# The output projection by seven half-size products, with six of the eight merges added by accumulating DMAs

## The chip, the cores and the metric

The kernel runs on one core of one Trainium2 chip. The metric is the device time of one execution in microseconds. TensorE (PE) multiplies, VectorE (DVE) and ScalarE (ACT) do elementwise work, GpSimd (POOL) does a little of it and issues some DMAs, SyncE (SP) only issues DMAs.

## The reference, cut to what matters

One decoder block on 512 tokens of 1024 channels, in float32. Two attention branches read the same normalised input; each is gated, projected to 1024 channels, scaled by a sigmoid gate, and the two are added. One more projection and the residual end it:

```
merged = (jax.nn.sigmoid(ga + b_gate[layer, 0]) * (y_fox @ w_fox[layer])
          + jax.nn.sigmoid(gb + b_gate[layer, 1]) * (y_moba @ w_moba[layer]))
x = x + merged @ w_out[layer]
```

The change concerns the second addend of `merged`, the sum of both, and the last line: a product of 512 x 1024 by 1024 x 1024.

## The kernel before, in words

**Precision.** Every large product is made of three: each operand is split into a high part (`hi`, rounded to the matmul's type by a copy on ACT) and a low part (`lo`, the difference, on DVE), and hi·hi, hi·lo and lo·hi are accumulated in PSUM. `split` (L131) does this for a weight chunk of 128 x 4 x 256 elements, with ACT at L134 and DVE at L136. Weight chunks come in by SP into four slots (`wr`), their parts live in four slots each (`wh`, `wl`).

**Stages.** After the input projections and the attention (until about 291 us) comes the gates stage. It makes the four blocks GA0, GA1, GB0 and GB1 of the sigmoid gates, each by seven products of half the size instead of eight (`group`, L703; the matmuls at L747 to L750 have 256 columns). The sums and differences of activations that this form needs were made earlier; those of weights are DVE subtractions at L711. Between these blocks the MoBA branch is projected: `unit_m` (L807), for i = 0 to 3 (weights wm0 to wm3) and c = 0 and 1, makes one tile j = 2i + c of 128 channels by 512 tokens with `br_mm` (L676 to L678, 12 matmuls of 512 columns). DVE multiplies it by its gate (L813), adds the other branch's gated tile `FS` (L814), ACT makes the high part (L819), DVE the low part (L820). These eight pairs `MG[j]` are the left operand of the output product.

**The output product.** `first_o` (L824) and `unit_o` (L838) multiply the merged tiles by w_out, in four groups of 256 columns (wo0 to wo3) and four tiles of 128 tokens, over 8 tiles of k, three matmuls each of 256 columns: L832 to L834 for the first group, L847 to L849 for the others. `out_o` (L853) loads the piece of x by SP, adds it on DVE (L857) and stores 128 x 256 elements by ACT's queue (L858). PSUM banks have names: `pj` (2), `tp` (3), `lg` (2), `pv` (1).

**The order.** The code is written in the order of the lists at its end (`order`, `seq`, `filler`); `pump` (L179) issues loads when a slot is free and splits weights three units ahead. The framework then orders each engine's instructions by that order and by a planner's costs: an instruction whose operands are not ready in its plan lets a later one of the same engine go first. So matmuls of the first output group stand between branch products in the trace. Each engine then works through its queue strictly in that order and waits where an operand is late. `tc.issue_after` puts instructions behind a given one of their engine. Tiles of a stage's pool lie where those of the stage before lay, and wait for the last user of these bytes.

Of the kernel before, what the change touches and what calls it, by code (L numbers as in the profile page):

```python
# [19 lines left out]
CW = 256  # L20
# [3 lines left out]
WR = 4  # L24
# [5 lines left out]
def fox_moba_kernel(ctx: ExitStack, tc, xT, x, w_in, w_fl, w_fox, w_moba, w_out, cst, rope, out):  # L30


    nc = tc.nc
    V, A, G, T = nc.vector, nc.scalar, nc.gpsimd, nc.tensor

    con = ctx.enter_context(tc.tile_pool(name="con", bufs=1))
    sb = ctx.enter_context(tc.tile_pool(name="sb", bufs=1))
# [3 lines left out]
    stage = {}  # L41
# [46 lines left out]
    cs = con.tile([P, C_END], F32, name="cs")  # L88
# [17 lines left out]
    for i in range(WARM):  # L106
# [10 lines left out]
    Gh = con.tile([P, KT, S], F32R, name="Gh")  # L117
    Gl = con.tile([P, KT, S], F32R, name="Gl")
# [10 lines left out]
    chunks = {}  # L129

    def split(src, n, name, half=False):  # L131
        hi = sb.tile([P, 4, 264], F32R, name=f"wh_{name}", tag="wh", bufs=4)
        lo = sb.tile([P, 4, 264], F32R, name=f"wl_{name}", tag="wl", bufs=4)
        A.activation(hi[:, :, 0:n], src, AF.Copy)  # L134
        for eng, q in ((V, slice(0, 2)), (G, slice(2, 4))) if half else ((V, slice(0, 4)),):
            eng.tensor_tensor(out=lo[:, q, 0:n], in0=src[:, q], in1=hi[:, q, 0:n].bitcast(F32), op=OP.subtract)  # L136
        return hi, lo
# [24 lines left out]
    COLS = {}  # L162
# [13 lines left out]
    loads, preps, first_prep = [], [], {}  # L176
    done = {"loads": 0, "preps": 0}

    def pump(i):  # L179

        while True:
            j = done["loads"]
            if j < len(loads) and (j < WR or loads[j - WR][1] < done["preps"]):
                loads[j][0]()
                done["loads"] += 1
            elif done["preps"] < len(preps) and done["preps"] <= i + 3:
                preps[done["preps"]]()
                done["preps"] += 1
            else:
                return  # L190

    def stream(name):
        first_prep[name] = len(preps)
        if name[0] == "G":
            group(name)
            return
        w, n, cnt = ((w_fox, int(name[2]), 1) if name[:2] == "wf" else (w_moba, int(name[2]), 1) if name[:2] == "wm"
                     else (w_out, int(name[2]), 2) if name[:2] == "wo" else (w_in, COLS[name] // CW, 2))
# [15 lines left out]
    r = con.tile([P, NT], F32, name="r")  # L214
# [33 lines left out]
    HT = S // 2  # L248
# [420 lines left out]
    FS, MG = {}, {}  # L669

    def br_mm(p, name, br, c):
        hi, lo = chunks[name][0]
        cc = slice(c * P, (c + 1) * P)
        for k in range(4):
            yh, yl = Y[br, k]
            T.matmul(p, hi[:, k, cc], yh, start=(k == 0), stop=False)  # L676
            T.matmul(p, hi[:, k, cc], yl, start=False, stop=False)  # L677
            T.matmul(p, lo[:, k, cc], yh, start=False, stop=(k == 3))  # L678
# [14 lines left out]
    SG = {}  # L693
# [7 lines left out]
    groups = {}  # L701
# [104 lines left out]

    def unit_m(i, c):  # L807
        def go():
            j = 2 * i + c
            p = pj(f"pm{j}")  # L810
            br_mm(p, f"wm{i}", "m", c)
            u = SG[i][:, c, :]
            V.tensor_tensor(out=u, in0=p, in1=u, op=OP.mult)  # L813
            V.tensor_tensor(out=u, in0=u, in1=FS[i][:, c, :], op=OP.add)  # L814
# [4 lines left out]
            A.activation(mh_, u, AF.Copy)  # L819
            V.tensor_tensor(out=ml_, in0=u, in1=mh_.bitcast(F32), op=OP.subtract)  # L820
            MG[j] = (mh_, ml_)
        return go

    def first_o():  # L824
        banks = [pst(tg, 2, f"po0_{i}") for i, tg in enumerate(("pj", "pj", "lg", "lg"))]
        for kk in range(KT):
            hi, lo = chunks["wo0"][kk // 4]
            gh, gl = MG[kk]
            k = kk % 4
            for t in range(NT):  # L830
                st = slice(t * P, (t + 1) * P)
                T.matmul(banks[t][:, :CW], gh[:, st], hi[:, k, :CW], start=(kk == 0), stop=False)  # L832
                T.matmul(banks[t][:, :CW], gh[:, st], lo[:, k, :CW], start=False, stop=False)
                T.matmul(banks[t][:, :CW], gl[:, st], hi[:, k, :CW], start=False, stop=(kk == KT - 1))  # L834
        for t in range(NT):
            out_o(banks[t], 0, t)

    def unit_o(n, t):  # L838
        def go():
            p = pj(f"po{n}{t}")  # L840
            st = slice(t * P, (t + 1) * P)
            for hf in range(2):
                hi, lo = chunks[f"wo{n}"][hf]
                for k in range(4):
                    kk = 4 * hf + k
                    gh, gl = MG[kk]
                    T.matmul(p[:, :CW], gh[:, st], hi[:, k, :CW], start=(kk == 0), stop=False)  # L847
                    T.matmul(p[:, :CW], gh[:, st], lo[:, k, :CW], start=False, stop=False)  # L848
                    T.matmul(p[:, :CW], gl[:, st], hi[:, k, :CW], start=False, stop=(kk == KT - 1))  # L849
            out_o(p, n, t)  # L850
        return go

    def out_o(p, n, t):  # L853
        xr = t2("pt", 4, "xr")[:, :CW]
        nc.sync.dma_start(out=xr, in_=x[t * P:(t + 1) * P, n * CW:(n + 1) * CW])
        o = t2("u", 4, "ot")
        V.tensor_tensor(out=o[:, :CW], in0=p[:, :CW], in1=xr, op=OP.add)  # L857
        nc.scalar.dma_start(out=out[t * P:(t + 1) * P, n * CW:(n + 1) * CW], in_=o[:, :CW])  # L858


    order = ["fqa", "fka", "fza", "fzb", "fva", "fqb", "fkb", "fvb", "mqa", "mka", "mva", "mza", "mqb", "mkb", "mvb", "mzb", "wf0", "wf1", "wf2", "wf3",
             "GA0", "GA1", "GB0", "wm0", "wm2",
             "GB1", "wm1", "wm3", "wo0", "wo1", "wo2", "wo3"]
    for nm in order[2:]:
        stream(nm)

    def units(name):
        k = name[:2]
        if k[0] == "G":
            return groups[name]  # L870
        if k == "wf":
            return [unit_f(int(name[2]), c) for c in range(2)]
        if k == "wm":
            return [unit_m(int(name[2]), c) for c in range(2)]
        if k == "wo":
            return [unit_o(int(name[2]), t) for t in range(4)]
# [28 lines left out]
    def seq(names):  # L905
        for u in filler(names):
            u()
# [32 lines left out]
    for n in range(4):  # L940
# [9 lines left out]
        if n == 0:  # L950
            for k in range(4):
                store = []

                at = 3 * k + 5
# [89 lines left out]
```

## Time and profile before

| | us |
|---|---|
| median of 3 runs | 432.96 (432.49 to 433.72) |
| the profiled execution, own time | 432.8 |
| its span, first to last instruction | 431.1 |
| busy in the span: PE, DVE, ACT, POOL | 424.4, 308.5, 253.9, 87.8 |
| last matmul issued | 427.3 |
| last branch matmul (wm3) issued | 383.7 |

The span leaves out what lies before the first and behind the last instruction, so it is 1.7 us shorter than the execution's own time. A matmul's duration in a row is that of one matmul through a pipeline and includes its drain; what matters is the distance between the starts of two in a row. In a row of a stage the granted clock of TensorE is given with 1.00 as full speed. A row of DMA issues ends with the size of one and the median time from issue to landing.

### The profile page before, as it was taken

What the parts mean: (1) busy time and instruction counts of PE and PEld (TensorE: products, weight loads), DVE (VectorE), ACT (ScalarE), POOL (GpSimd) and SP (SyncE); (2) the same over time, 40 slices, a digit from 0 to 9 for tenths busy, and PEclk for the clock granted to TensorE, in tenths of its full rate; (3) what the DMA queues carried; (4) which work ended last, traced back from release to release, by engine and by line L of the source; (5) the groups of instructions that cost most, each with busy time, mean ns of one, the idle gap of its engine ahead of it and who ended that gap; (6) DMA issues with size and microseconds to landing.
All of it is one profiled execution on the core that took longest, in us unless ns stands there. A gap on an engine that the chain in (4) does not pass through costs nothing.

```text
span 431.1 us, 8090 instructions
## 1 busy us (share of the span) xinstructions
PE 424.4 (98%) x3103; PEld 400.7 (93%) x3103; DVE 308.5 (72%) x551; ACT 253.9 (59%) x488; POOL 87.8 (20%) x108
## 2 busy tenths in 40 slices
PE   8999999999999999999999999999999999999996
PEld 6998899999999998999998888899999989999996
DVE  5669976869979867767856896859897796673311
ACT  4986336876867867667765876647645545531100
POOL 1049200227044650045630103020000000000000
PEclk9999999999999999999999999999999999999999
DMA  7981235236565414304304305271415206525231
GB/s 239 398 296 57 80 116 152 74 103 205 166 209 185 130 45 123 122 3 126 117 15 136 109 13 200 99 263 51 141 55 196 98 2 210 189 95 166 85 94 45
DMA packets 25670, 56.13 MB, mean 130 GB/s; under 512 B 3240, under 2 KB 11872, under 8 KB 25632
## 3 DMA queue, kind: packets, MB, share of 16 engines
q1 hardware_dynamic: 14528, 40.08, 27.8%
q10 hardware_dynamic: 9952, 11.34, 8.8%
q0 software_dynamic: 1152, 4.19, 2.7%
q8 instruction: 24, 0.39, 0.4%
q14 instruction: 14, 0.11, 0.1%
HBM read 46.01 MB, written 6.32 MB: 121 GB/s over the span
## 4 chain that ended last, share of the span: by engine, by line
PE 84%; DVE 7%; DMA 5%; ACT 2%; issue 1%; SPq 1%; DVEq 0%; ACTq 0%
PE pb_GB L750 3%; PE pb_GA L750 3%; PE pb_GA L747 3%; PE pb_GB L749 3%; PE pb_GB L747 3%; PE pb_GA L749 3%; PE po L847 3%; PE po L849 3%; PE po L848 3%; PE pv L608 2%; PE pv L607 2%; PE lg L553 2%; PE lg L552 2%; PE pm L676 2%; PE pm L677 2%; PE pm L678 2%
## 5 line engine op out<-in xcount | busy, mean ns | idle before, releaser
L331 POOL TENSOR_TENSOR ff<-ss,mh 128x8 f32<-128x8 f32 x16 | 28.6, 1793 | 65.6 <-DVE ss L329 65.1
L557 ACT ACTIVATE p<-p,negm 128x128 f32<-128x128 f32 (+1 forms) x64 | 35.7, 559 | 9.7 <-DVE negm L555 8.2
L555 DVE CUSTOM_DVE_ANT_0 p<-lg,mask 128x128 f32<-128x128 f32 (+1 forms) x64 | 30.9, 485 | 14.4 <-PE lg L553 13.7
L847 PE MATMUL po<-wh_wo,mgh 128*128 128x256 f32 x96 | 27.1, 282 | 0.0
L849 PE MATMUL po<-wh_wo,mgl 128*128 128x256 f32 x96 | 27.0, 282 | 0.0
L848 PE MATMUL po<-wl_wo,mgh 128*128 128x256 f32 x96 | 27.0, 281 | 0.0
L857 DVE TENSOR_TENSOR ot<-po,xr 128x256 f32<-128x256 f32 x16 | 6.6, 424 | 24.7 <-PE po L849 23.5
L136 DVE TENSOR_TENSOR wl_GA<-wr_ga,wh_GA 128x1024 fp32r<-128x1024 f32 x14 | 17.9, 1294 | 5.7 <-ACT wh_GA L134 3.6
L134 ACT ACTIVATE wh_wo<-wr_wo 128x1024 fp32r<-128x1024 f32 x8 | 8.5, 1061 | 21.6 <-PE po L849 8.0
L552 PE MATMUL lg<-KH,QS 128*128 128x128 f32 (+1 forms) x64 | 20.5, 329 | 0.0
L134 ACT ACTIVATE wh_GA<-wr_ga 128x1024 fp32r<-128x1024 f32 x14 | 14.6, 1059 | 9.2 <-PE pb_GA L749 4.6
L136 DVE TENSOR_TENSOR wl_GB<-wr_gb,wh_GB 128x1024 fp32r<-128x1024 f32 x14 | 16.8, 1222 | 4.2 <-ACT wh_GB L134 3.3
L134 ACT ACTIVATE wh_GB<-wr_gb 128x1024 fp32r<-128x1024 f32 x14 | 14.6, 1060 | 8.6 <-PE pm L677 2.5
L633 DVE TENSOR_TENSOR ypair<-pv,ysh 64x512 f32<-64x512 f32 x16 | 11.0, 688 | 11.2 <-ACT ysh L632 11.0
L847 PEld LDWEIGHTS po<-wh_wo,mgh 128*128 128x128 f32 x96 | 18.1, 189 | 0.0
L848 PEld LDWEIGHTS po<-wl_wo,mgh 128*128 128x128 f32 x96 | 18.1, 189 | 0.0
L849 PEld LDWEIGHTS po<-wh_wo,mgl 128*128 128x128 f32 x96 | 18.1, 188 | 0.0
L136 DVE TENSOR_TENSOR wl_wo<-wr_wo,wh_wo 128x1024 fp32r<-128x1024 f32 x8 | 9.8, 1222 | 7.4 <-ACT wh_wo L134 7.4
L604 DVE TENSOR_TENSOR ptl<-p_a,pth 128x512 fp32r<-128x512 f32 x16 | 11.0, 686 | 4.7 <-ACT pth L603 4.7
L526 DVE SCALAR_TENSOR_TENSOR QS<-p_qT,cs,QS 64x512 fp32r<-64x512 f32 x16 | 12.0, 750 | 2.5 <-ACT QS L525 2.1
L750 PE MATMUL pb_GA<-Gh,wl_GA 128*128 128x256 f32 x48 | 13.6, 283 | 0.0
L749 PE MATMUL pb_GA<-Gl,wh_GA 128*128 128x256 f32 x48 | 13.5, 281 | 0.0
(447 smaller groups left out, 1764.5 us busy)
## 6 DMA issues: line engine op xcount, KB each, us to landing
wr_ga<-in_w_in_dram SPq DMA_DIRECT2D x8, 512.0 KB, 3.5
wr_gb<-in_w_in_dram SPq DMA_DIRECT2D x8, 512.0 KB, 4.1
wr_wo<-in_w_out_dram SPq DMA_DIRECT2D x8, 512.0 KB, 3.8
xt<-in_xT_dram SPq DMA_DIRECT2D x8, 256.0 KB
x<-in_x_dram SPq DMA_DIRECT2D x8, 256.0 KB, 7.5
KH<-KH ACTq DMA_DIRECT2D x16, 128.0 KB, 2.4
s_dramh<-sum_sh ACTq DMA_DIRECT2D x8, 256.0 KB
s_draml<-sum_sl ACTq DMA_DIRECT2D x8, 256.0 KB, 3.5
```

The costliest lines, as they stand in the source:

```text
L134: A.activation(hi[:, :, 0:n], src, AF.Copy)
L136: eng.tensor_tensor(out=lo[:, q, 0:n], in0=src[:, q], in1=hi[:, q, 0:n].bitcast(F32), op=OP.subtract)
L331: G.tensor_tensor(out=f2, in0=ss.rearrange("p t h -> p (t h)"), in1=mh, op=OP.pow)
L552: T.matmul(lg[:, :n], qs[:, qt], kh[:, :n], start=True, stop=False)
L555: V.tensor_tensor_reduce(pt, lg[:, :n], mask[:, 512 - n:512], -0.125, 3.0e38, op0=OP.add, op1=OP.min, accum_out=mkn[:, hh, i:i + 1])
L557: A.activation(pt, pt, AF.Exp, bias=mkn[:, hh, i:i + 1], scale=-1.0, accum_out=rs[:, hh, i:i + 1])
L747: T.matmul(o, hi[:, k, cc], lh, start=(n < 3 and c == 0 and k == 0), stop=False, skip_group_check=True)
L749: T.matmul(o, hi[:, k, cc], ll, start=False, stop=False, skip_group_check=True)
L750: T.matmul(o, lo[:, k, cc], lh, start=False, stop=(k == 3), skip_group_check=True)
L847: T.matmul(p[:, :CW], gh[:, st], hi[:, k, :CW], start=(kk == 0), stop=False)
L848: T.matmul(p[:, :CW], gh[:, st], lo[:, k, :CW], start=False, stop=False)
L849: T.matmul(p[:, :CW], gl[:, st], hi[:, k, :CW], start=False, stop=(kk == KT - 1))
```

## The change

The output product is made in blocks. The merged tiles, as a matrix of tokens by channels, fall into four blocks A11 to A22 (256 tokens by 512 channels), w_out into B11 to B22 (512 by 512). Seven block products replace eight, with sums of left blocks S1 = A21 + A22, S2 = S1 - A11, S4 = A12 - S2, S3 = A11 - A21 and, of weights, T1 = B12 - B11, T3 = B22 - B12, T2 = B22 - T1 and T4 = B21 - T2. Each product is two tiles of 128 tokens, four of k, three matmuls of 512 columns.

- **Merges.** For wm0, wm1 and wm2 the other branch's tile is added by a DMA from GpSimd's queue that accumulates onto the tile in SBUF; for wm3 DVE adds as before. For j < 4 only the first 256 tokens are split into hi and lo (`merge_b`), for j > 3 all 512.
- **Left sums.** `sum_o` makes each sum on DVE for two tiles at once (512 elements), m = 0 from wm0 and wm2, m = 1 from wm1 and wm3; `parts_o` splits it on ACT and DVE into the space of `Gh` and `Gl`, the normalised input's parts, which the gates stage read last.
- **Weights.** Each block is two chunks of 128 x 1024. B11 and B21 come through the `wr` slots, B22 and B12 into the last stage's pool. T1 and T3 are made by a negation on ACT and an accumulating DMA from DRAM; T2 and T4 by DVE subtractions. `prep(n)` splits the weights of product n.
- **Results.** `keep` copies a partial result from PSUM by ACT and adds x to it by an accumulating DMA (128 x 512); `result` adds it to another PSUM bank on DVE and stores 512 columns by ACT's queue; the last tile goes in two halves, the second stored by SP.
- **Order.** The tail is written out by hand, with `behind()` holding some splits and subtractions behind the last DVE instruction.

```diff
-            V.tensor_tensor(out=u, in0=u, in1=FS[i][:, c, :], op=OP.add)
-            if i % 2:
-                mh_, ml_ = (stage["pool"].tile([P, S], F32R, name=f"mg{hl}{j}", tag="mg", bufs=8) for hl in "hl")
...
+            if i == 3:
+                V.tensor_tensor(out=u, in0=u, in1=FS[i][:, c, :], op=OP.add)
             else:
-                mh_, ml_ = (t2("y", 15, f"mg{hl}{j}", dt=F32R) for hl in "hl")
-            A.activation(mh_, u, AF.Copy)
-            V.tensor_tensor(out=ml_, in0=u, in1=mh_.bitcast(F32), op=OP.subtract)
+                G.dma_start(out=u, in_=FS[i][:, c, :], accum_op=OP.add)
+
+    def merge_b(i, c):
...
+            n = HT if j < 4 else S
...
+            A.activation(mh_, u[:, 0:n], AF.Copy)
+            V.tensor_tensor(out=ml_, in0=u[:, 0:n], in1=mh_.bitcast(F32), op=OP.subtract)
             MG[j] = (mh_, ml_)
...
+    def parts_o(m, what):
+        f = SF[m, what]
+        hi, lo = (so(what, q)[:, 2 * m:2 * m + 2, :] for q in range(2))
+        A.activation(hi, f, AF.Copy)
+        V.tensor_tensor(out=lo, in0=f, in1=hi.bitcast(F32), op=OP.subtract)
...
+    O_PRODUCTS = (("A11", "11", 1), ("A12", "21", 2), ("S4", "22", 4), ("S3", "T3", 3), ("S2", "T2", 1),
+                  ("S1", "T1", 1), ("A22", "T4", 3))
...
+        def minus(key, c, plus):
+            A.activation(R[key, c], R[key, c], AF.Copy, scale=-1.0)
+            G.dma_start(out=dst(key, c), in_=src(plus, c), accum_op=OP.add)
...
+                A.activation(wide(hi), wide(R[key, c]), AF.Copy)
+                V.tensor_tensor(out=wide(lo), in0=wide(R[key, c]), in1=wide(hi).bitcast(F32), op=OP.subtract)
...
+                if n == 0:
+                    minus("11", c, "12")
...
+        def late_loads():
+            for key in ("22", "12"):
+                for c in range(2):
+                    load(key, c, stage["pool"])
+            for c in range(2):
+                minus("12", c, "22")
...
+            for t in range(2):
+                o = b[at][t].rearrange("p (n c) -> p n c", n=2)
                 for k in range(4):
...
+                    T.matmul(o, gh, hi[:, :, r, :], start=(new and k == 0), stop=False, skip_group_check=True)
+                    T.matmul(o, gh, lo[:, :, r, :], start=False, stop=False, skip_group_check=True)
+                    T.matmul(o, gl, hi[:, :, r, :], start=False, stop=(k == 3), skip_group_check=True)
...
+                A.activation(e[at][:, t, :], b[at][t], AF.Copy)
+                t0 = tq * HT + t * P
+                G.dma_start(out=e[at][:, t, :], in_=x[t0:t0 + P, cq * 512:(cq + 1) * 512], accum_op=OP.add)
...
+                    V.tensor_tensor(out=o[:, c:c + n], in0=b[bb][t][:, c:c + n], in1=e[ee][:, t, c:c + n], op=OP.add)
+                    eng = nc.scalar if c == 0 else nc.sync
+                    eng.dma_start(out=out[t0:t0 + P, cq * 512 + c:cq * 512 + c + n], in_=o[:, c:c + n])
...
-    seq(["wm1", "wm3"])
-    pump(first_prep["wo0"])
-    first_o()
-    seq(["wo1", "wo2", "wo3"])
+    groups["WO"]()
...
+        m1[0]()
+        prep(0)
+        m1[1]()
+        for what in ("S1", "S2", "S4", "S3"):
+            sum_o(0, what)
+        merge_b(1, 0)
+        m3[0]()
...
+        merge_b(1, 1)
+        prep(1)
+        prep(2, (0,))
+        m3[1]()
...
+        merge_b(3, 0)
+        product(0)
+        evac(0)
+        merge_b(3, 1)
+        for what in ("S1", "S2", "S4"):
+            sum_o(1, what)
+        with behind():
+            prep(2, (1,))
+        parts_o(1, "S4")
+        product(1)
...
+        product(5)
+        result(1, 4, 0, 1)
+        result(1, 3, 1, 1)
+        product(6)
+        evac(6)
```

More of the change, by code (lines that the diff above doesn't have):

```diff
@@ L808, in go, with merge_a @@
         def go():
+            merge_a(i, c)
+            merge_b(i, c)
+        return go
+    def merge_a(i, c):
+        if True:
             j = 2 * i + c
@@ L822, in unit_m @@
[L822 to L843, printed above, removed]
-                for k in range(4):
[L845 to L851, printed above, removed]
@@ new lines, in merge_b @@
+    def merge_b(i, c):
+        if True:
+            j = 2 * i + c
+            u = SG[i][:, c, :]
+            n = HT if j < 4 else S
+            tiles = [stage["pool"].tile([P, S], F32R, name=f"mg{j}{q}", tag="mg", bufs=6) if i % 2
+                     else t2("y", 15, f"mg{j}{q}", dt=F32R) for q in range(n // HT)]
+            mh_, ml_ = (tiles[0][:, 0:HT], tiles[0][:, HT:S]) if j < 4 else tiles
+            A.activation(mh_, u[:, 0:n], AF.Copy)
+            V.tensor_tensor(out=ml_, in0=u[:, 0:n], in1=mh_.bitcast(F32), op=OP.subtract)
+            MG[j] = (mh_, ml_)
@@ new lines, in fox_moba_kernel, with so, sum_o @@
+    O_AT = {"S3": (0, HT), "S1": (0, 0), "S2": (4, 0), "S4": (4, HT)}
+    def so(what, hl):
+        k, c = O_AT[what]
+        return (Gh, Gl)[hl][:, k:k + 4, c:c + HT]
+    SF = {}
+    def sum_o(m, what):
+        a, b = SG[m], SG[m + 2]
+        x, y, op = {"S1": (a[:, :, HT:S], b[:, :, HT:S], OP.add), "S2": (SF.get((m, "S1")), a[:, :, 0:HT], OP.subtract),
+                    "S4": (b[:, :, 0:HT], SF.get((m, "S2")), OP.subtract),
+                    "S3": (a[:, :, 0:HT], a[:, :, HT:S], OP.subtract)}[what]
+        f = SF[m, what] = stage["pool"].tile([P, S], F32, name=f"so_{what}{m}", tag="sf", bufs=4).rearrange("p (k t) -> p k t", t=HT)
+        V.tensor_tensor(out=f, in0=x, in1=y, op=op)
@@ L861, in fox_moba_kernel @@
     order = ["fqa", "fka", "fza", "fzb", "fva", "fqb", "fkb", "fvb", "mqa", "mka", "mva", "mza", "mqb", "mkb", "mvb", "mzb", "wf0", "wf1", "wf2", "wf3",
              "GA0", "GA1", "GB0", "wm0", "wm2",
-             "GB1", "wm1", "wm3", "wo0", "wo1", "wo2", "wo3"]
+             "GB1", "wm1", "wm3", "WO"]
     for nm in order[2:]:
@@ L873, in units @@
         if k == "wm":
-            return [unit_m(int(name[2]), c) for c in range(2)]
-        if k == "wo":
-            return [unit_o(int(name[2]), t) for t in range(4)]
+            i = int(name[2])
+            return [unit_m(i, c) if i % 2 == 0 else (lambda c=c: merge_a(i, c)) for c in range(2)]
         if k[1] == "z":
@@ L978, in fox_moba_kernel, with behind @@
     enter("end")
-    seq(["wm1", "wm3"])
-    pump(first_prep["wo0"])
-    first_o()
-    seq(["wo1", "wo2", "wo3"])
+    groups["WO"]()
+    prep, product, evac, sub, result = (groups[k] for k in ("prep", "product", "evac", "sub", "out"))
+    def behind():
+        return tc.issue_after(last_on(mybir.EngineType.DVE))
+    m1, m3 = filler(["wm1"]), filler(["wm3"])
+    if True:
+        m1[0]()
[5 more added lines that the diff above has]
+        m3[0]()
+        parts_o(0, "S4")
+        parts_o(0, "S3")
+        merge_b(1, 1)
+        prep(1)
+        prep(2, (0,))
+        m3[1]()
+        parts_o(0, "S2")
+        parts_o(0, "S1")
+        pump(10 ** 6)
+        merge_b(3, 0)
[8 more added lines that the diff above has]
+        product(1)
+        sum_o(1, "S3")
+        parts_o(1, "S3")
+        prep(3)
+        product(2)
+        evac(2)
+        with behind():
+            sub("22", "22", "11")
+            parts_o(1, "S2")
+        evac(1)
+        prep(4)
+        product(3)
+        evac(3)
+        with behind():
+            parts_o(1, "S1")
+            prep(5)
+        product(4)
+        evac(4)
+        with behind():
+            sub("21", "21", "22")
+        prep(6)
+        product(5)
[3 more added lines that the diff above has]
+        evac(6)
     stage.pop("guard").__exit__(None, None, None)
```

84 lines of the change are left out of this document (77 added, 7 removed).

## The prediction

> **What bounds the kernel now.** I read the page's busy shares, then the busy time by stage, then the output product by itself.
>
> ```profile
> span 431.1 us, 8090 instructions
> PE 424.4 (98%) x3103; PEld 400.7 (93%) x3103; DVE 308.5 (72%) x551; ACT 253.9 (59%) x488; POOL 87.8 (20%) x108
> PE 84%; DVE 7%; DMA 5%; ACT 2%; issue 1%; SPq 1%; DVEq 0%; ACTq 0%
> 300.00:340.00 40.00, 40.00 (x328) 39.45 (x327) 32.62 (x32) 22.94 (x32) 0.00 (x0) 1.00 0.39 132
> 371.00:384.00 13.00, 13.00 (x77) 11.43 (x76) 8.86 (x12) 4.78 (x8) 0.00 (x0) 1.00 0.51 163
> 384.00:427.50 43.50, 43.43 (x367) 43.23 (x365) 13.97 (x24) 5.80 (x6) 0.00 (x0) 1.00 0.29 95
> ```
>
> The third line is the chain that ended last, by engine. The stage rows give bounds and length, then busy time of PE, weight loads, DVE, ACT and POOL, then the granted clock (1.00), DMA share and GB/s. TensorE never waits in the stages that the change touches: 13.00 of 13.00 us around the last branch products, 43.43 of 43.50 in the output product. So only less matmul time makes the kernel faster, and any new TensorE wait costs its full length. The row 300:340 is the gates stage, which already makes seven products of half size with hi/lo splits beside them: PE 40.00 of 40.00 with DVE at 32.62 and ACT at 22.94.
>
> **The matmuls removed and added.** The same view for the tile po alone, and the last branch product with the first output matmul behind it:
>
> ```profile
> 371.00:384.00 13.00, 2.75 (x19) 2.79 (x20) 0.00 (x0) 1.00 0.51 163
> 384.00:427.50 43.50, 43.43 (x366) 43.23 (x365) 6.21 (x16) 1.00 0.29 95
> 381.11 0.40 PE L676 MATMUL pm<-yhm,wh_wm 128*128 128x512 f32 x1
> 383.66 0.39 PE L678 MATMUL pm<-yhm,wl_wm 128*128 128x512 f32 x1
> 383.89 0.28 PE L832 MATMUL po<-wh_wo,mgh 128*128 128x256 f32 x1
> ```
>
> Before, 4 column groups x 4 token tiles x 8 k x 3 products of hi and lo are 384 matmuls of 256 columns. They hold PE for 2.75 + 43.43 = 46.2 us, 0.120 us each. After, 7 products x 2 token tiles x 4 k x 3 are 168 matmuls of 512 columns. The trace has that shape in the branch product: 12 of them start between 381.11 and 383.66 and the next instruction at 383.89, so one takes 2.78 / 12 = 0.232 us. The output then needs 168 x 0.232 = 39.0 us, **7.2 us less**. The columns fall to 7/8 (5.8 us); the rest is the wider form, 0.232 for 512 against twice 0.120.
>
> On this price the Trainium skill ("TensorE: Matmul & The Clock Gate", Back-to-back issue gap) speaks against the change: N/2.4 + 2.5 ns for an isolated matmul. That would be 216 and 109 ns, so 41.9 - 36.3 = 5.6 us gained and about 1.6 us less than by the rows; the trace's intervals are longer than both and decide.
>
> **The end.** Now the last instruction is an addition of 256 columns, then the store:
>
> ```profile
> 427.15 0.28 PE L849 MATMUL po<-wh_wo,mgl 128*128 128x256 f32 x1
> 427.47 0.42 DVE L857 TENSOR_TENSOR ot<-po,xr 128x256 f32<-128x256 f32 x1 [2.44 <-PE po L849]
> 427.93 0.34 ACTq L858 DMA_DIRECT2D out_dram<-ot  x1
> ```
>
> The new end adds two halves of 256 columns, each stored by itself on ACT and SP. The first is today's tail; the second addition costs some 0.35 us more (0.42 less its overlap). **Plus 0.35 us.**
>
> **What is added on DVE and ACT.** Groups: count, then busy us and mean ns of one.
>
> ```profile
> L136 DVE TENSOR_TENSOR wl_wo<-wr_wo,wh_wo 128x1024 fp32r<-128x1024 f32 x8 | 9.8, 1222 | 7.4 <-ACT wh_wo L134 7.4
> L711 DVE TENSOR_TENSOR wr_gb<-wr_gb,wr_gb 128x1024 f32<-128x1024 f32 x8 | 9.8, 1220 | 0.6 <-DMA wr_gb<-in_w_in_dram 0.6
> L134 ACT ACTIVATE wh_wo<-wr_wo 128x1024 fp32r<-128x1024 f32 x8 | 8.5, 1061 | 21.6 <-PE po L849 8.0 <-DVE ot L857 4.9 <-issue 3.4
> L857 DVE TENSOR_TENSOR ot<-po,xr 128x256 f32<-128x256 f32 x16 | 6.6, 424 | 24.7 <-PE po L849 23.5 <-PE po L834 1.2
> L814 DVE TENSOR_TENSOR uGB<-uGB,f 128x512 f32<-128x512 f32 x8 | 5.5, 689 | 0.1
> L819 ACT ACTIVATE mgh<-uGB 128x512 fp32r<-128x512 f32 x8 | 5.0, 631 | 11.0 <-DVE uGB L814 11.0
> ```
>
> DVE gains 14 weight low parts and 4 weight subtractions (18 x 1.22 = 22.0 us), 8 sums and 8 low parts of sums (16 x 0.69 = 11.0) and the results (7 x 0.69 + 2 x 0.42 = 5.7): 38.7. It loses 8 weight low parts (9.8), 16 output additions (6.6), 6 merge additions (4.1) and the half-width of 4 merge low parts (1.1): 21.6. Net 17 us. From 371 on DVE is busy 8.9 + 14.0 = 22.8 us; 40 us in the some 50 us left is 80%, about the 82% (32.62 of 40.00) that the gates stage carries with no TensorE wait. ACT gains 6 weight copies, 4 negations, 8 copies of sums and 8 of banks, about 19 us, and stands near 30 of 50 us. These run beside the matmuls, so I cost them at nothing; if that cover fails, every microsecond by which a product's operands are late is one of TensorE idle (third rival).
>
> The double buffers bear this out. A weight half has a slot when its predecessor two products back is done, some 7.0 us before it is needed (one product 24 x 0.232 = 5.6, and a quarter of one), against 1.06 + 1.22 for its split.
>
> **What is added on GpSimd's queue: 18 accumulating DMAs**, 6 merges of 256 KB inside the chip's SBUF, 4 of 512 KB that finish weight differences, 8 of 256 KB that add x. The trace shows no accumulating DMA, only neighbours: plain copies by the same queue, copies within SBUF by ACT's, the queue's total (packets, MB, share of the 16 DMA engines' span), and one issue.
>
> ```profile
> S1h<-s_dramh POOLq DMA_DIRECT2D x1, 512.0 KB, 3.5
> S3h<-s_dramh POOLq DMA_DIRECT2D x1, 512.0 KB, 6.3
> KH<-KH ACTq DMA_DIRECT2D x16, 128.0 KB, 2.4
> q0 software_dynamic: 1152, 4.19, 2.7%
> 263.34 0.54 POOL L279 DMA_DIRECT2D S0l<-s_draml  x1
> ```
>
> Landing of one 256 KB addition: not under 2.4 us (half the bytes, no addition); at the upper end 6.3 us for the slowest copy, plus what stands ahead of it in the same queue. 2.7% of 431.1 us for 4.19 MB is 360 GB/s, 1.45 us for 512 KB, and, as an addition must also read its destination, I estimate 2.9 us. I take **5.0 us**, the middle of the eight copies (3.5 to 6.3), whose 512 KB are what an addition of 256 KB reads and writes on its own side. GpSimd itself is idle in the stage rows above (0.00), and 18 issues of 0.54 us are 9.7 us. But it takes them in order: an addition that waits for its operand holds back all behind it, and an ACT copy that waits for a merge holds back ACT's weight copies and thereby DVE's low parts.
>
> Only the merges of wm1 are close. Rows of DVE: the last wm2, the second wm1 and the last wm3 product:
>
> ```profile
> 352.52 0.69 DVE L813 TENSOR_TENSOR uGB<-pm,uGB 128x512 f32<-128x512 f32 x1 [0.38 <-PE pm L678]
> 376.73 0.69 DVE L813 TENSOR_TENSOR uGB<-pm,uGB 128x512 f32<-128x512 f32 x1 [0.17 <-PE pm L678]
> 384.09 0.69 DVE L813 TENSOR_TENSOR uGB<-pm,uGB 128x512 f32<-128x512 f32 x1 [0.63 <-PE pm L678]
> 384.81 0.69 DVE L814 TENSOR_TENSOR uGB<-uGB,f 128x512 f32<-128x512 f32 x1
> ```
>
> The factor is ready at 377.4. TensorE's other work (both wm3 products and the 12 matmuls of product 0 with k = 0 and 1, which fill as long as today's 2.75 us of output matmuls) lasts to 383.9; k = 2 takes 6 x 0.232, so k = 3 is wanted at 385.3. Between lie the issue (0.54), ACT's copy (0.45, estimated as less than 0.63 for half the width), DVE's low part (0.42) and some 0.3 of handovers: the landing may take **6.2 us** without a stall. With 5.0 there is none; behind one 512 KB addition it is 7.9 and costs 1.7. I allow **1.3 us**, near the upper end, since the weight additions are issued in the same microseconds.
>
> The merges of wm0 and wm2 have their factor by 353.2 and over 20 us until product 0. The merges of wm3, added by DVE as now, end at 385.5; then the low parts of a weight half (1.22) and of the merge (0.69) end near 387.4, wanted by product 1 at 383.9 + 12 x 0.232 + 9 x 0.232 = 388.8. S4 takes three sums, a copy and a low part more, near 391, wanted at 393.6.
>
> **The sum**, against the profiled execution's 432.8 us (span 431.1; the median of the runs, 432.96, is 0.16 above): 432.8 - 7.2 + 0.35 + 1.3 = 427.25, and with the 0.16 a median of **427.4 us**.
>
> **Rivals.** *The additions stand in line* (430.7). GpSimd's single queue has the four 512 KB weight additions in the same 10 us as wm1's merges. Behind two of them a merge lands after 5.0 + 2 x 2.9 = 10.8, TensorE idles 4.6 us: 426.1 + 4.6. For: weights and merges become ready together between 371 and 378. Against: GpSimd's slots are assigned as operands become ready. By the Trainium skill ("DMA: Bandwidth & Descriptors", Issuing engines are not separate DMA queues) all issuers share one set of engines, so the weight loads beside them would lengthen this further; here 371:384 shows these at 0.51.
>
> *DVE and ACT are late product by product* (430.5). Product 1 has 1.4 us of slack, the others 2 to 4. If two more 1.22 us operations fall ahead of an operand at product 1 and at two later ones, that is 1.0 and about 1.0 each, 3 us over the 427.4. Against it: the gates stage.
>
> *Slower: accumulating DMAs far slower than copies* (436.5). From a landing of 6.2 + 6.85 = 13.1 us on, the stall eats the whole gain (7.2 - 0.35); over 14.4 it is slower beyond noise. Behind four additions of 2.9 us, or two at half that speed, it is 16.6: a stall of 10.4 us, 426.1 + 10.4. For: no run here prices an addition. Against: even the slowest copy took 6.3.
>
> That the matmuls are not cheaper is excluded by the pm rows, which have the same shape, types and loads.
>
> **Chances.** Forecast 0.50 (own range 425.7 to 428.9: no stall, less 0.4 of scatter, to 2.8 of stall); additions in line 0.17 (428.9 to 432.5); DVE and ACT late 0.10; slow additions 0.21, of which 0.05 below the noise bound; better still 0.02. A measurement here tells 0.3%, or 1.3 us, from no change: faster (below 431.7) 0.50 + 0.02 + 0.15 + 0.10 = 0.77, same 0.02 + 0.05 = 0.07, slower (above 434.3) 0.16. The range runs to 434.2 so that only 0.02 + 0.16 stay outside.
>
> **What would show it.** Right: 168 matmuls of 512 columns at 0.232 us; PE idle after the last pm product under 2 us; the six merge additions landing in 4 to 6 us. In line: ACT's copy of the third and fourth merged tiles waits for a DMA, and PE with it. DVE late: PE waits for a low part of weights or sums at products 1 to 6. Wrong altogether if landings exceed 13 us, or PE idles over 7 us before the end.

## The result and the profile after

The changed kernel takes **429.84 us** (median of 4 runs, 429.33 to 430.48) against 433.32 (4 runs) on the same chip: ratio 0.9923, 95% interval 0.9901 to 0.9944. A second set of runs of the same kernel gave 430.1 (ratio 0.9931, 0.9916 to 0.9947). So it is faster, by about 3.3 us, and not by the forecast 5.5.

First the head of the page, the busy times by stage (bounds, length, then PE, weight loads, DVE, ACT, POOL, granted clock, DMA share, GB/s) and the same for the tile `po`.

```profile
span 428.8 us, 7677 instructions
PE 419.6 (98%) x2887; PEld 386.7 (90%) x2887; DVE 324.3 (76%) x564; ACT 270.8 (63%) x514; POOL 106.1 (25%) x126
```

```profile
371.00:384.00 13.00, 13.00 (x70) 11.06 (x69) 7.17 (x10) 5.69 (x10) 2.12 (x2) 1.00 0.94 257
384.00:427.50 43.50, 39.24 (x166) 30.37 (x164) 34.62 (x44) 22.78 (x32) 11.51 (x12) 1.00 0.69 140
371.00:378.00 7.00, 7.00 (x44) 6.19 (x43) 5.04 (x7) 3.53 (x6) 2.12 (x2) 1.00 0.96 305
378.00:384.00 6.00, 6.00 (x28) 4.87 (x27) 2.13 (x4) 2.16 (x4) 0.00 (x0) 1.00 0.90 200
```

```profile
402.50:424.50 22.00, 22.00 (x96) 17.60 (x95) 4.54 (x7) 3.42 (x6) 1.00 0.71 157
```

TensorE has 216 matmuls fewer (3103 before) and works 4.8 us less. But in 384 to 427.5, where it idled 0.07 us before, it now shows 39.24 of 43.50: some of that is the earlier end, some are holes. And the DMA share between 371 and 384 is 0.94, where the same stretch before showed 0.51. Now the holes, as TensorE's waits after 340 us and ACT's longest one (who waited for whom, us in total, times, longest):

```profile
PE po L941 <- ACT mg L837: 0.9, 1, 0.9
PE pb_GB L750 <- ACT e_GB L760: 0.6, 1, 0.6
PE po L941 <- ACT wh_o L904: 0.4, 1, 0.4
PE po L942 <- DVE wl_o L905: 0.2, 1, 0.2
```

```profile
ACT mg L837 <- DMA uGB<-f: 15.3, 4, 5.1
```

A row's wait counts from the modelled end of the matmul before, drain included. What a hole costs is the distance between two starts, less the usual spacing. Measured so, after 300 us, the holes are 0.87 at 360.6 (in the gate block GB1), 0.69 at 385.3, 1.18 at 392.9, 0.52 at 400.8 and 0.09 more: **3.35 us, against 0.00 before**. This sum of holes is given for each kernel below. ACT's line shows the origin: four of its copies of merged tiles wait 15.3 us for the accumulating DMAs.

The merges of wm1, in order, on POOL, ACT, DVE and PE (start, us, instruction, in brackets the idle time ahead of it and what ended it):

```profile
373.25 0.86 POOL L826 DMA_DIRECT2D uGB<-f  x1 [17.96 <-DVE uGB L822]
373.90 1.47 POOL L891 DMA_DIRECT2D wr_o<-in_w_out_dram  x1
384.54 1.20 POOL L891 DMA_DIRECT2D wr_o<-in_w_out_dram  x1 [9.18 <-ACT wr_o L890]
385.29 1.38 POOL L826 DMA_DIRECT2D uGB<-f  x1
```

```profile
381.84 0.42 ACT L837 ACTIVATE mg<-uGB 128x256 fp32r<-128x256 f32 x1 [5.06 <-DMA uGB<-f]
383.21 1.04 ACT L890 ACTIVATE wr_o<-wr_o 128x1024 f32<-128x1024 f32 x1
392.43 0.94 ACT L837 ACTIVATE mg<-uGB 128x256 fp32r<-128x256 f32 x2 [2.40 <-DMA uGB<-f]
```

```profile
382.29 0.43 DVE L838 TENSOR_TENSOR mg<-uGB,mg 128x256 fp32r<-128x256 f32 x1 [3.78 <-ACT mg L837]
384.03 0.68 DVE L822 TENSOR_TENSOR uGB<-pm,uGB 128x512 f32<-128x512 f32 x1
```

```profile
392.90 0.50 PE L941 MATMUL po<-wh_o,mg 128*128 128x512 f32 x1 [0.92 <-ACT mg L837]
```

The first addition is issued at 373.25 and has landed when ACT's copy starts at 381.84. The trace's answer for this one issue (duration in ns, then its time to landing):

```profile
L826 POOL DMA_DIRECT2D uGB<-f x1: 859/859/859, 373.2 to 373.2; - x1
DMA to landing us min/median/max: 8.6/8.6/8.6
```

The second, issued at 385.29, takes 7.1 us in the same view, the four of wm0 and wm2 3.3 to 4.0. The two late ones had different company. Until about 378 SP's weight loads fill the DMA engines beside the first. When the second is issued the loads are done (from 384.5 to 392.5 the trace has no packet of SP's queue), but a weight addition of 512 KB was issued 0.75 us ahead of it in GpSimd's own queue.

The wait is passed on: ACT's copy holds the negation at 383.21 behind it, which holds a weight addition on POOL (384.54), which stands ahead of the second merge; on DVE the low part of the first merge (382.29) stands ahead of the multiplication (384.03) that the second merge needs. TensorE ends up waiting at 392.90. The holes at 385.3 and 400.8 end with the high and the low part of a weight half (`wh_o`, `wl_o`), made by ACT and DVE behind such waits.

### The profile page after: what moved, and what is told of

Same layout as the page of the kernel before. It is cut to its first block, busy times and chain, and to the rows that moved or that the text cites. A ratio compares the mean times of both kernels' runs of the same rounds, so it can differ in the third digit from the quotient of the medians.

```text
span 428.8 us, 7677 instructions
## 1 busy us (share of the span) xinstructions
PE 419.6 (98%) x2887; PEld 386.7 (90%) x2887; DVE 324.3 (76%) x564; ACT 270.8 (63%) x514; POOL 106.1 (25%) x126
## 4 chain that ended last, share of the span: by engine, by line
PE 72%; issue 9%; DVE 8%; DMA 8%; ACT 1%; POOL 0%; SPq 0%; DVEq 0%; POOLq 0%; ACTq 0%
DMA x<-in_x_dram 3%; PE pb_GA L753 3%; PE pb_GA L750 3%; PE pb_GA L752 3%; DMA xt<-in_xT_dram 3%; PE pv L611 2%; PE pv L610 2%; PE lg L556 2%; PE lg L555 2%; PE po L943 2%; PE po L942 2%; PE po L941 2%; PE pb_GB L750 2%; PE pb_GB L752 2%; PE p_b L600 2%
## 5 line engine op out<-in xcount | busy, mean ns | idle before, releaser
L826 POOL DMA_DIRECT2D uGB<-f x6 | 5.8, 961 | 84.3 <-issue 56.1
L905 DVE TENSOR_TENSOR wl_o<-wr_o,wh_o 128x1024 fp32r<-128x1024 f32 x14 | 16.9, 1222 | 2.9 <-ACT wh_o L904 2.8
L904 ACT ACTIVATE wh_o<-wr_o 128x1024 fp32r<-128x1024 f32 x14 | 14.7, 1055 | 6.5 <-PE po L943 2.9
L837 ACT ACTIVATE mg<-uGB 128x256 fp32r<-128x256 f32 (+1 forms) x8 | 4.1, 521 | 16.2 <-DMA uGB<-f 15.3
L635 ACT ACTIVATE ysh<-pv 64x512 f32<-64x512 f32 x16 | 9.5, 593 | 7.1 <-PE pv L611 4.5
L753 PE MATMUL pb_GB<-Gh,wl_GB 128*128 128x256 f32 x48 | 13.5, 281 | 0.0
L750 PE MATMUL pb_GA<-Gh,wh_GA 128*128 128x256 f32 x48 | 13.5, 281 | 0.0
L750 PE MATMUL pb_GB<-Gh,wh_GB 128*128 128x256 f32 x48 | 13.5, 280 | 0.0
L752 PE MATMUL pb_GB<-Gl,wh_GB 128*128 128x256 f32 x48 | 13.4, 280 | 0.0
```

Of the source, the lines that this page charges most:

```text
L750: T.matmul(o, hi[:, k, cc], lh, start=(n < 3 and c == 0 and k == 0), stop=False, skip_group_check=True)
L752: T.matmul(o, hi[:, k, cc], ll, start=False, stop=False, skip_group_check=True)
L753: T.matmul(o, lo[:, k, cc], lh, start=False, stop=(k == 3), skip_group_check=True)
L904: A.activation(wide(hi), wide(R[key, c]), AF.Copy)
L905: V.tensor_tensor(out=wide(lo), in0=wide(R[key, c]), in1=wide(hi).bitcast(F32), op=OP.subtract)
```

## The experiments

Two theories were set against each other. **The additions are late and in-order queues pass this on** (the cause is where they run: shared DMA engines and the queues), or **DVE and ACT are late with the new work** whoever adds the merges. Beside these stood the question whether an accumulating DMA is slow in itself. All kernels compute the whole result. "Holes" is the sum described above.

| kernel | median us | ratio to before, 95% interval | holes |
|---|---|---|---|
| the change again | 430.1 | 0.9931 (0.9916 to 0.9947) | 3.36 |
| wm1's merges by DVE | 427.96 | 0.9882 (0.9862 to 0.9901) | 0.88 |
| all merges by DVE | **427.79** | 0.9876 (0.9856 to 0.9896) | 0.00 |
| late loads held back | 428.74 | 0.9895 (0.9876 to 0.9913) | 1.57 |
| the additions alone, old product | 436.45 | 1.0090 (1.0075 to 1.0106) | 5.06 |
| all merges by DVE, 256 columns | 428.22 | 0.9894 (0.9881 to 0.9907) | 0.00 |
| all eight merges by DMA | 436.71 | 1.0100 (1.0077 to 1.0123) | 9.27 |
| weight differences by DVE | 432.83 | 1.0000 (0.9989 to 1.0011) | 5.49 |
| wm1: DVE's order changed | 430.26 | 0.9946 (0.9929 to 0.9963) | 3.10 |
| wm1: DVE's and GpSimd's order | 428.87 | 0.9908 (0.9891 to 0.9925) | 1.79 |

In the kernels with the new product, the time less its holes is 426.7 to 428.2 us, with holes from 0.00 to 9.27. So the holes account for the differences, but only to within some 1.5 us: they are those of one profiled execution each, and in these executions the gate block GB0, which stands ahead of all merges, begins anywhere between 313.5 and 314.9.

**The change again**, for the runs beside it.

> The changed kernel again, as a reference for the runs on this chip. All theories: 429.3 to 430.5 us, ratio to before near 0.992; TensorE idle about 0.9 us in GB1's products, 0.7 and 1.2 us in product 0, 0.5 us in product 2.

It gave 430.1, with holes of 3.36 at the same places: they belong to the kernel, not to one execution.

**All merges by DVE, and wm1's alone.**

```diff
-            if i == 3:
+            if i >= 0:          # wm1's alone: if i in (1, 3)
                 V.tensor_tensor(out=u, in0=u, in1=FS[i][:, c, :], op=OP.add)
```

> All eight merges by DVE, none by DMA; the seven products unchanged. If the additions by DMA cost the idle time, GB1's 0.9 us goes as well as product 0's 1.9 us: about 427.1 us, near the 426.1 us of the sum without any stall. If they save more DVE time than they cost in waits, 430.5 to 432 us.

> The merges of wm1 go back to DVE; those of wm0 and wm2 stay additions by DMA. If late landings of wm1's two additions (8.6 and 7.1 us) cause the idle time before and in product 0, some 1.9 us go and the stall of 0.9 us in GB1's products stays: about 428.0 us. If DVE is short of time instead, its two more additions (2 x 0.69 us) make it the same or up to 1.2 us slower: 429.8 to 431.0 us.

With all merges on DVE no TensorE wait is left after 340 us, and 427.79 is below the change itself, with intervals that do not meet (0.9856 to 0.9896 against 0.9916 to 0.9947 in the same set of runs). DVE carries six additions more and still has room: PE, weight loads, DVE and ACT by stage in this kernel:

```profile
371.00:384.00 13.00, 13.00 (x70) 11.06 (x69) 11.71 (x17) 10.73 (x16) 2.75 (x3) 1.00 0.96 257
384.00:427.50 43.50, 38.05 (x164) 30.38 (x162) 30.73 (x39) 17.32 (x25) 9.14 (x10) 0.96 0.59 122
```

(The clock of 0.96 comes from behind the last matmul, which starts at 421.66: it is 1.00 up to 424 and 0.52 from there on.) Against the change, DVE is busier before 384 (11.71 against 7.17) and less afterwards (30.73 against 34.62): the work has moved to where there was room. The theory that DVE and ACT are late by themselves falls here. With wm1's merges alone on DVE one hole stays, the one in GB1 (its row of waits reads as in the change, 0.6 us of wait). So wm1's additions make 2.48 of the 3.35 us of holes, wm2's the other 0.87. In medians the two kernels do not differ (427.96 and 427.79).

**Late loads held back.** The weight blocks B22 and B12 (four loads of 512 KB) are issued only once wm1's first addition has been issued. A one-column memset on GpSimd, later overwritten by the load, stands between:

```diff
+                if pool is not sb:
+                    with tc.issue_after(last_on(mybir.EngineType.Pool)):
+                        G.memset(R[key, c][:, 0, 0:1], 0.0)
                 nc.sync.dma_start(out=dst(key, c), in_=src(key, c))
...
-    groups["WO"]()
...
         m1[0]()
+        groups["WO"]()
```

> The four late weight loads (B22 and B12, 512 KB each) start only behind wm1's first merge, held by a one-column memset that they overwrite. If the DMA engines that all queues share are what delays that merge's addition (share 0.96 from 371 to 378 us), it lands within 3.3 to 5 us of its issue instead of 8.6, and 1 to 1.9 us of idle time go: 428 to 429 us. If an addition is slow in itself or stands in GpSimd's queue, it lands as late as before and the time is 429.8 us or more.

The first and the second of wm1's additions in this kernel, then its DMA load by stage:

```profile
L826 POOL DMA_DIRECT2D uGB<-f x1: 859/859/859, 373.3 to 373.3; - x1
DMA to landing us min/median/max: 3.3/3.3/3.3
```

```profile
L826 POOL DMA_DIRECT2D uGB<-f x1: 888/888/888, 381.0 to 381.0; - x1
DMA to landing us min/median/max: 9.0/9.0/9.0
```

```profile
371.00:378.00 7.00, 7.00 (x44) 6.19 (x43) 5.04 (x7) 4.75 (x9) 2.31 (x6) 1.00 0.62 109
378.00:384.00 6.00, 6.00 (x28) 4.87 (x27) 5.65 (x9) 4.82 (x7) 2.09 (x2) 1.00 1.06 324
384.00:388.00 4.00, 4.00 (x19) 3.24 (x18) 2.92 (x4) 1.34 (x2) 0.88 (x1) 1.00 1.10 262
```

Issued at the same microsecond as in the change (373.3), the same addition lands after 3.3 us instead of 8.6. The second, now beside the loads that were moved and 1.6 us behind a weight addition (379.40), takes 9.0. (The share adds up the time of all packets, so it can pass 1.) The first merge's lateness goes with the loads. An accumulating DMA is not slow in itself.

**Weight differences by DVE.** The four weight additions on GpSimd's queue are replaced by DVE subtractions, the weight loads stay:

```diff
-                if n == 0:
-                    minus("11", c, "12")
...
-            for c in range(2):
-                minus("12", c, "22")
...
+        sub("11", "12", "11")
         prep(2, (0,))
...
+        sub("12", "22", "12")
         prep(3)
```

> The changed kernel with T1 and T3 made by DVE subtractions instead of a negation and an addition by DMA: GpSimd's queue then holds only the merges and x, and 2 MB less are moved. If standing behind the 512 KB additions in that queue is what delays wm1's merges, both land near 3.3 us and the idle time of product 0 goes: 428 us. If the plain weight loads do it, wm1's first addition still lands near 8 us and only the second comes sooner: 429 to 430 us.

With no other addition in GpSimd's queue, wm1's first merge still lands only after 8.2 us, beside the weight loads (DMA share 0.95 from 371 to 378). The second, at 383.9 with the loads done (0.38 from 384 to 388), lands after 3.3. So for the first one the weight loads are enough; a line of additions in GpSimd's queue is not its cause. For the second one that line is: with no weight addition ahead of it 3.3 us, with one 7.1 in the change. The kernel itself is back at 432.83, the time of before, which neither theory expected. Its DVE has no room left at the end:

```profile
388.00:396.00 8.00, 7.08 (x32) 5.42 (x31) 7.96 (x11) 3.15 (x5) 0.00 (x0) 1.00 0.01 2
396.00:403.00 7.00, 5.55 (x22) 3.63 (x21) 7.00 (x10) 4.22 (x8) 1.73 (x2) 1.00 0.47 75
```

DVE is busy 7.96 of 8.00 and 7.00 of 7.00 us, and TensorE waits for it, directly or by way of ACT's copies of what DVE made. The rival of a late DVE is real, then, but four operations of 1.22 us away; and the accumulating DMAs that make weight differences do earn their place, unlike those of the merges.

**What holds the second merge of wm1.** In the change two queues stand ahead of it. First only DVE's order is changed, so that the multiplication at 384.03 goes ahead of the low part; then GpSimd's too, so that the weight additions of T1 come behind both merges.

```diff
         m1[1]()
+        c1 = last_on(mybir.EngineType.DVE)
+        with tc.issue_after(last_on(mybir.EngineType.Pool)):   # second kernel only:
+            groups["add"]()                                    # the T1 additions, out of prep(0)
...
-        merge_b(1, 0)
+        with tc.issue_after(c1):                               # the parts_o(0, ...) too
+            merge_b(1, 0)
```

> The second merge of wm1 has its product from TensorE near 378.6 us, but its multiplication on DVE runs at 384.03 and its addition is issued at 385.29. Two things stand in front of it: on DVE the low part of the first merge, which waits for ACT; on GpSimd a weight addition, whose negation on ACT stands behind the same copy. Here only the order of DVE is changed: the multiplication comes ahead of the low part. Theory (both queues hold it): the multiplication moves to 379 to 380, the addition stays at 384.9 to 385.4, TensorE's idle stays near 3.3 us and the time within 0.4 of 430.1. Rival (DVE's order alone holds it): the addition is issued near 380, the 1.18 us of idle near 392.9 goes, and the time is 428.9. Second rival (the transfers are late in any order): no change in time, and the addition, issued near 380, lands after 390.

> As the kernel with the multiplication ahead on DVE, and in GpSimd's queue the two additions that finish T1 = B12 - B11 stand behind both merges of wm1; nothing is added or left out. Theory (both queues hold the second addition): it is issued near 380, lands by 387 to 388 beside the last weight loads, the idle of 1.18 us near 392.9 goes, and the time is 428.9 (428.4 to 429.4); of the idle about 2.2 us stays, at the first merge and at GB1. Rival (the shared transfers alone make it late): it lands after 390 though issued near 380, and the time stays within 0.4 of 430.1. Rival (the weight additions become late in turn): TensorE waits for T1's parts at the fifth product, and the time is 430 or more.

DVE's order alone: the multiplication, then GpSimd.

```profile
377.63 0.69 DVE L822 TENSOR_TENSOR uGB<-pm,uGB 128x512 f32<-128x512 f32 x1
```

```profile
382.61 1.21 POOL L891 DMA_DIRECT2D wr_o<-in_w_out_dram  x1 [8.23 <-ACT wr_o L890]
383.35 1.38 POOL L826 DMA_DIRECT2D uGB<-f  x1
```

The operand is there at 378.3, and the addition is issued at 383.35, behind a weight addition that waited for ACT. That is earlier than expected, but this execution is ahead from the start of the stage on, and its first addition landed after 7.6 us: between the issues of the two merges lie 11.1 us (372.26 to 383.35), in the change 12.0. The time is 430.26, as the change. With both orders changed:

```profile
373.40 0.86 POOL L826 DMA_DIRECT2D uGB<-f  x1 [17.95 <-DVE uGB L822]
379.76 0.86 POOL L826 DMA_DIRECT2D uGB<-f  x1 [5.49 <-DVE uGB L822]
380.40 1.47 POOL L984 DMA_DIRECT2D wr_o<-in_w_out_dram  x1
```

```profile
390.43 0.40 ACT L837 ACTIVATE mg<-uGB 128x256 fp32r<-128x256 f32 x1
```

Now it is issued at 379.76, with the weight addition behind it, lands after 4.9 us, and the time is 428.87. The theory of both queues holds, in the size that it gave (428.9); of the holes 1.79 us stay, where it had 2.2. Two limits: GpSimd's order alone was not run, and the interval (0.9891 to 0.9925) is clear of that of DVE's order alone (0.9929 to 0.9963, same set of runs), not of that of the change (0.9916 to 0.9947, another set). ACT's copy of this tile no longer waits for a DMA (no bracket), but it starts at 390.43 behind other copies in ACT's queue, and 0.61 us of the hole stays. (The framework also moved the split of one weight half by a place or two on ACT and DVE.)

**The additions alone.** The kernel before, with six of its eight merges as accumulating DMAs and nothing else:

```diff
-            V.tensor_tensor(out=u, in0=u, in1=FS[i][:, c, :], op=OP.add)
+            if i == 3:
+                V.tensor_tensor(out=u, in0=u, in1=FS[i][:, c, :], op=OP.add)
+            else:
+                G.dma_start(out=u, in_=FS[i][:, c, :], accum_op=OP.add)
```

> The kernel before with one part of the change alone: the merges of wm0, wm1 and wm2 added by DMA, the output product as before. If ACT's copy waiting for an addition stalls TensorE in GB1's products whatever follows, about 0.9 us are lost there: 434.0 us or a little more, since the output product of before has matmuls to fill product 0's waits. If the additions relieve DVE of something that matters, 432.5 us or less.

This half of the change is 0.9% slower by itself (1.0075 to 1.0106), 2.4 us more than the 434.0 expected from GB1's hole alone. The first hole is the one in GB1 again; the largest stands in the first output group, and behind it something else shows. TensorE around the hole, then the stages behind it with the granted clock in the third column from the end:

```profile
387.54 0.38 PE L835 MATMUL po<-wh_wo,mgh 128*128 128x256 f32 x1 [1.86 <-ACT mgh L822]
388.59 0.28 PE L836 MATMUL po<-wl_wo,mgh 128*128 128x256 f32 x1
388.71 0.28 PE L837 MATMUL po<-wh_wo,mgl 128*128 128x256 f32 x1
...
389.22 0.41 PE L837 MATMUL po<-wh_wo,mgl 128*128 128x256 f32 x1
389.43 0.41 PE L835 MATMUL po<-wh_wo,mgh 128*128 128x256 f32 x1
```

```profile
386.00:388.00 2.00, 0.46 (x3) 0.46 (x4) 0.48 (x1) 0.63 (x1) 0.00 (x0) 1.00 0.74 270
388.00:390.00 2.00, 2.00 (x15) 2.00 (x14) 1.85 (x4) 1.09 (x2) 0.00 (x0) 0.71 0.04 8
390.00:391.50 1.50, 1.50 (x9) 1.50 (x8) 1.47 (x3) 0.49 (x1) 0.00 (x0) 0.50 0.00 0
391.50:393.00 1.50, 1.50 (x12) 1.50 (x11) 1.50 (x3) 0.63 (x1) 0.00 (x0) 0.74 0.00 0
```

About 1.3 us after the hole of 2.0 us the distance between starts goes from 0.12 to 0.21 us, while the granted clock falls to 0.50, and it has recovered by about 393. The sum of holes counts this slower spacing too, here some 1.5 of the 5.06 us, and so it does in the next kernel.

**All eight merges by DMA** (`if i == 9` in the place of `if i == 3`).

> The changed kernel with the merges of wm3 by DMA too: the suspected wait taken to all eight. The last addition can be issued only when the last wm3 product is done, 9 matmuls of product 1 (2.1 us) and what is left of product 0 (some 5 us) ahead of its use, and S4's sums wait for it as well. With a landing of 3.3 us undisturbed, 7 to 9 beside other transfers, and the copies and sums behind it, 3 to 7 us of idle time more than the changed kernel: 433 to 437 us. If landings don't matter: 429.8 us.

436.71 us, slower than before by 1.0% (1.0077 to 1.0123). Here the additions of wm3 stand directly ahead of TensorE (the longer of these two waits; the other is for wm1's second merge, as in the change):

```profile
PE po L941 <- ACT mg L837: 3.9, 2, 2.7
```

The slower rival's outcome exists, then: not by one addition of over 13 us, but by additions without slack, and with a clock at 0.50 between 400 and 402.

**256 columns.** All merges by DVE, each matmul of 512 columns made as two of 256:

```diff
-                    T.matmul(o, gh, hi[:, :, r, :], ...)
+                    for n2 in range(2):
+                        T.matmul(o[:, n2], gh, hi[:, n2, r, :], ...)
```

> All merges by DVE and seven products, but each matmul of 512 columns made as two of 256 with the same weights: 336 instead of 168. If the wide form is worth what the intervals say (168 x 0.2315 against 336 x 0.118 us), it is 0.8 us slower than with wide matmuls, about 428.6 us; by the prediction's 0.120 us per matmul 1.4 us, about 429.2 us. If TensorE does not set the time there, the same 427.8 us.

428.22 against 427.79: 0.43 us in medians, and the intervals overlap (0.9881 to 0.9907 and 0.9856 to 0.9896), so this alone doesn't settle it. In the traces, both without holes, the stretch from the first matmul of GB0 to the last of the kernel is 0.77 us longer (107.57 and 106.80).

## Why the prediction was right or wrong

The sign and the range held; the median is 2.4 us above the forecast. But 429.84 lies outside the forecast's own range (425.7 to 428.9) and inside that of the rival *additions in line* (428.9 to 432.5): the stated range held because it took the rivals in. The two main terms were off in the same direction, so nothing cancelled. By the sum's terms:

**The matmuls (7.2 us) were mis-sized by 0.7.** The term was built from PE's busy time, and 2.75 + 43.43 us counts the drain of matmuls that stand between others. By starts, the 366 matmuls before that begin between 383.89 and 427.15 are 43.26 / 365 = 0.1185 us apart, 45.5 for all 384. After, the 96 that the row 402.5 to 424.5 counts, the first of them started at 402.32 and the last at 424.43, are 22.11 / 95 = 0.233 apart, 39.1 for 168. That is 6.4 less. The kernel without holes says the same: its stretch from GB0's first matmul to the end is 106.80 us, before 113.27, so 6.47. By the trace 5.7 of it is columns and 0.8 the wider form; the forecast had 5.8 and 1.4. The rule of the Trainium skill that was weighed there ("TensorE: Matmul & The Clock Gate", Back-to-back issue gap) gave, as an estimate, 5.6, of which 168 times 2.5 ns, or 0.4, for the wider form. The measured gain lies about midway between it and the forecast.

**The end (0.35 us) held.**

```profile
424.43 0.39 PE L943 MATMUL po<-wh_o,mg 128*128 128x512 f32 x1
424.86 0.76 DVE L959 TENSOR_TENSOR ot<-po,eo 128x256 f32<-128x256 f32 x2 [1.35 <-PE po L943]
```

From the last matmul to the end of the span it is 428.8 - 424.43 = 4.37 us, before 431.1 - 427.15 = 3.95: 0.42 more.

**The stall (1.3 us) was 3.35**, and three steps behind it failed.

*The landing of 5.0 us.* In the change no addition that fed a hole took that. Undisturbed it is 3.3 us, shorter than I took. wm1's first took 8.6 beside the weight loads. Its second took 7.1 behind one 512 KB addition; for that case the prediction had 7.9, and its 1.3 us lies between no stall (at 5.0) and 1.7 (at 7.9). For the first I had taken the DMA share of 0.51 for 371 to 384 from the profile of before. But in the change SP issues all eight weight loads of 512 KB in one go just ahead of that stretch, and the share there became 0.94 (0.96 from 371 to 378, where these loads are nearly all of it; before, 0.63):

```profile
363.12 9.17 SPq L887 DMA_DIRECT2D wr_o<-in_w_out_dram  x8
```

The trace agrees with what the Trainium skill says of this ("DMA: Bandwidth & Descriptors", Issuing engines are not separate DMA queues): all issuers share one set of engines (GpSimd's addition takes 8.6 us beside SP's loads, 3.3 with half of them held back). I quoted it against the forecast, and then priced it with the old load.

*The deadline of 6.2 us for the second merge*, which assumed that its factor is ready at 377.4 and its addition issued then. It was issued at 385.29. The prediction named the queues ("an addition that waits for its operand holds back all behind it, and an ACT copy that waits for a merge holds back ACT's weight copies") and didn't apply this to the step itself. The kernels with changed orders show that DVE's queue alone does not explain it, and that both together do: 430.26 with DVE's released, 428.87 with both.

*The merges of wm0 and wm2 at nothing, for over 20 us of slack.* The slack is that of their data. But ACT, in order, waits for wm2's addition at its place in the queue, ahead of a copy that TensorE wants at once:

```profile
358.51 0.63 ACT L837 ACTIVATE mg<-uGB 128x512 fp32r<-128x512 f32 x1 [3.92 <-DMA uGB<-f]
359.05 1.05 ACT L134 ACTIVATE wh_GB<-wr_gb 128x1024 fp32r<-128x1024 f32 x1
360.00 0.57 ACT L760 ACTIVATE e_GB<-pb_GB 128x512 f32<-128x512 f32 x1
```

```profile
360.63 0.38 PE L750 MATMUL pb_GB<-S1h,wh_GB 128*128 128x256 f32 x1 [0.61 <-ACT e_GB L760]
```

An addition of only 4.0 us costs 0.87 us of TensorE there, in a stage in which the forecast expected no stall.

**DVE and ACT at nothing: right.** DVE was put at 40 us from 371 on, and shows 7.17 + 34.62 = 41.8; ACT at 30, and shows 28.5. With the merges back on DVE there is no hole, so the new work is hidden.

**The rivals.** *Additions in line* was right for the second merge. One weight addition ahead of it in GpSimd's queue delayed its issue, by waiting for ACT, and then its landing (7.1 us, and 3.3 in the kernel without weight additions). The first merge stood behind nothing; its lateness is that of the weight loads on the shared engines, which this rival had as an aside. The prediction's own signs spoke for this rival too: ACT's copies of the third and fourth merged tiles waited for a DMA and TensorE with one of them, and only one of the six additions (4.0 us) landed in 4 to 6. *Slower* did not come: the longest landing of a merge in any run here is 9.0 us.

With the measured terms the sum is 432.8 - 6.4 + 0.42 + 3.35 = 430.2, and 429.84 was measured.

## What to carry to other kernels

Price a transfer with the DMA load that the change itself makes, not with that of the profile before, and with what stands ahead of it in its own queue. Where DVE has a spare microsecond in the very stage, let it make an addition rather than a DMA: here the seven products bring the gain, and the six additions by DMA give 2.0 to 2.3 us of it back (429.84 and 430.1 against 427.79; 3.35 by the holes). Slack belongs to a place in an in-order queue, not to the data: for each new wait read down the waiting engine's queue, then down the queue of whoever waits for that. Look for the engine with room in the very stage, as DVE had before 384 us and had no longer from 388 on.

## What was unexpected of the hardware

- One accumulating DMA of 256 KB within SBUF lands in 3.3 us when the engines are free, in 7.6 to 8.9 beside the weight loads (DMA share from 371 to 378 between 0.75 and 1.01) and in 7.1 with a 512 KB addition issued 0.75 us ahead of it in the same queue. Its issue is a row of 0.86 us on GpSimd, where that of the plain copy in the profile before is 0.54. Rows of issues overlap: at 385.29 it is 1.38 us long while the row of 384.54 (1.20) still runs, and the two starts are 0.75 us apart.
- After a TensorE hole of 2.0 us (additions alone) the granted clock fell to 0.50 for a time, and likewise between 400 and 402 in the kernel with all eight by DMA, behind a hole of 3.0 us that ended at 398.20. The one with weight differences by DVE has 5.49 us of holes in pieces of at most 1.2, and its clock stays at 1.00. So one long wait costs more than its length, in the first case by some 1.5 us. The Trainium skill ("TensorE: Matmul & The Clock Gate", Part 1: The HAM clock gate) tells of the halved clock after at least one idle window of about 3.4 us; the value agrees, but here 2.0 us of idle were enough. Why, no run here shows.
